# Deferred VectorE work queued behind the low part of its pair of k-blocks, in a hybrid attention and convolution block

## The chip, the cores and the metric

The kernel runs on one core of one Trainium2 chip. The metric is device time in microseconds of that core, from the start of an execution to its end; the median of three runs before the change is 2037.59 us (2037.36 to 2040.66). The engines that matter here are TensorE (PE in the profile: matrix products and transposes; PEld is its weight load), VectorE (DVE: elementwise work), ScalarE (ACT: casts and activations), the DMA queue that SyncE issues (SP) and GpSimd (POOL).

## The reference, cut to what matters

The input has 256 rows and 4096 columns. The projection `w_in` has 14336 columns: q, k, v and z_a (2048 each) for 16 attention heads, and a_c, g_c and z_c (2048 each) for a convolution module.

```python
xn = rms_norm(h, norm_in_g[i])
proj = xn @ w_in[i]
q, k, v, z_a, a_c, g_c, z_c = jnp.split(proj, ...)
y_a = chunked_attention(q, k, v, rel_table[i])
y_a = rms_norm(y_a, attn_out_g[i]) * silu(z_a)
u = a_c * sigmoid(g_c)                      # GLU
u = causal_depthwise_conv(u, w_dw, 31 taps) + b_dw
u = silu(layer_norm(u, ln_g, ln_b))
y_c = u @ w_pw + b_pw
y_c = rms_norm(y_c, conv_out_g[i]) * silu(z_c)
h = h + concatenate([y_a, y_c]) @ w_out[i]
gate = sigmoid(rms_norm(h, ple_norm_g[i]) @ w_ple_gate[i] + b_ple_gate[i])
h = h + gate * (p[i] @ w_ple[i])
out = rms_norm(h, final_g)
```

Everything is float32. The chip's products are made of two parts of each operand, high and low.

## The kernel before

**One k-block of a weight.** A k-block is 128 rows of a weight matrix, loaded as a tile `wt` of 128 x 1024 (two blocks of 512 columns). `parts_of` (lines 199 to 210) makes two operands of it: ScalarE casts `wt` to the high part `wh` (line 204), and VectorE subtracts to get the low part `wl` (line 205). The last pair of instructions made in this way is remembered in the list `recent` (line 209): its first entry is the cast on ScalarE, its second the subtraction on VectorE. There are three buffers each for `wh` and `wl`, and five for `wt`.

**A product.** `mixed_product` (lines 339 to 500) makes two blocks of 512 output columns at once and goes over the 16 pairs of k-blocks in an order written out by hand. A plain pair (no mark) costs VectorE two low parts of 1024 columns, and TensorE 24 matmuls (two k-blocks, two column blocks, two row halves, three part combinations). A pair marked `*` is done with seven products in place of eight, which is 21 matmuls, and needs sums of weight blocks: VectorE makes a low part of 512 columns for `w0`, two additions into `ua` (lines 464, 465), the low part `ul` of `ua`, the low part of `w1`, two more additions into `ub` (lines 471, 472) and the low part of `ub`. In a pair marked `+` the first two additions are made by the DMA on its way in. The products of a seven-pair accumulate in four more PSUM banks (`acc_P`), which are taken from the pool of temporary banks from the first seven-pair to the last.

**Deferred work.** VectorE work that nothing needs at once is put into the queue `later` (line 180) as closures. At the end of every pair, `fill(n)` (lines 182 to 184) takes the next n closures and traces their instructions there; n comes from a list, `fills`, indexed by the pair's place in the order. I say that a closure is *dealt* to the pair after which `fill` traces it. What goes through `later`:

- the convolution: `glu_conv(c)` queues 4 x 31 = 124 taps, each one VectorE instruction on up to 256 columns (lines 714 and 718), for c = 0 to 3, 496 in all. The 31 taps of one channel block are a chain, as each adds to the same `cv`;
- `combinations(c)`: two closures, one of five VectorE instructions (lines 291 and 268 to 271) and one of a cast and a subtraction (lines 276, 277);
- `layer_norm_swish`: sums, means, centring (line 799), squares (line 803 on ScalarE, their additions on line 807), the scaling (line 832), the activation and the split into parts (line 844);
- the gating of `y_a` and `y_c` (line 1031, recorded as line 184), a combination of the last output operand, and, in the gate's products, the multiplication of the embedding's product with the gate, the addition to `hc`, its square (ScalarE) and its weighting (lines 1155 to 1158; recorded as line 184).

**The order of the stages**, with the closures dealt in each: `glu_conv(0)`; then for g = 0, 1, 2: `glu_conv(g + 1)` and `heads(g)`; then `layer_norm_swish` (which only queues) and `heads(3)`. `heads(g)` is a product for q and k, one for v (`product`, lines 235 to 247, fills of 2 at each of 16 pairs), then `attention(g)`, whose small matmuls, softmax and transposes are spread among the first pairs of the next product. The products of `glu_conv(1)`, `glu_conv(2)` and of q and k use

```python
early = units("1 3 5 0+ 7 9 2+ 11 13 4+ 15 8 6+ 10 12 14")
early_fills = (5, 6, 1, 5, 6, 1, 5, 6, 1, 5, 6, 1, 2, 5, 5, 4)
```

(q and k of `heads(3)` with a fill of 4 at every pair), and the product of `glu_conv(3)`, called the last a/g product below, uses

```python
early_six = units("1 3 5 7 0* 9 2* 11 4* 13 6* 15 8* 10* 12 14")
six_fills = (4, 6, 7, 1, 5, 1, 5, 1, 5, 1, 2, 4, 6, 6, 6, 4)
```

where `more_combinations` also puts two combinations at the head of `later`, ahead of pairs 7 and 9. Both lists add up to 64. After the attention come the pointwise product (fills of 0), the z products and `w_out` (2) and the gate's products (4), whose orders are written out in the same way and are mostly `*` pairs.

**What sets the order on an engine.** The order of the instructions on each engine is fixed when the program is built. The framework goes through a list schedule: of the instructions whose inputs it reckons to be there, an engine takes the one traced first. So a closure dealt to a late pair may be placed far ahead of that pair on VectorE, if its inputs are there and nothing traced earlier is. `pin` (line 89) holds an instruction behind the one traced before it on its engine; `queued_behind` (lines 214 to 220) holds what is traced inside it behind given instructions, each on its own engine: an edge of order, not a wait for the other's end. Before the change only the parts of `ua` in `+` pairs use it (line 466), with what `recent` held when the pair began. Each engine executes its instructions in the order so fixed.

Of the kernel before, what the change touches and what calls it, by code (L numbers as in the profile page):

```python
# [25 lines left out]
def hybrid_block(  # L26
# [24 lines left out]
    _, T, D = x.shape  # L51
# [128 lines left out]
    later = deque()  # L180

    def fill(n):
        for _ in range(min(n, len(later))):
            later.popleft()()


    def weight_parts(w, col, k0, kc, tiles=None):
# [24 lines left out]
    recent = []  # L212
# [126 lines left out]
    def mixed_product(  # L339
        w, col, lhs, comb, order, on_helpers, ahead=None, fills=(0,), on_begin=None, apart=NB,  # L340
        left=(), begin=None,
    ):

        c = [[ps_acc.tile([P, NB], F32, tag="acc", name=f"acc{h}{j}") for j in range(2)] for h in range(NH)]  # L350
        helper = {}
        begun, ends = set(), {}
        n_left = len(left) // 2
        for n, (_, seven) in enumerate(order[: len(order) - n_left]):
            for name in ("P1", "P5", "P6", "P7", "P2", "P3", "P4") if seven else ("P2", "P3", "P4", "X"):
                ends[name] = n
        banks = {"P2": c[0][0], "P3": c[0][1], "P4": c[1][0], "X": c[1][1]}
        made, held = [], []

        def add_left(h, js, out=None, cols=slice(None)):  # L360


            for m in range(0, len(held), 2):
                for j in js:
                    dst = c[h][j] if out is None else out[:, cols]
                    for i, (kb, (wh, wl)) in enumerate(held[m : m + 2]):
                        xh, xl = block(kb, h)
                        for kind, (a, b) in enumerate(((xh, wh), (xl, wh), (xh, wl))):
                            pin(
                                nc.tensor.matmul(  # L370
                                    dst, a, b[:, j, cols],
                                    start=out is not None and m + i + kind == 0,
                                    stop=m + i + 1 == len(held) and kind == 2,
                                )
                            )

        def add(name, x, w2, n, final, kinds=range(3), then=lambda ins: None):

            for kind in kinds:
                a, b = ((x[0], w2[0]), (x[1], w2[0]), (x[0], w2[1]))[kind]  # L380
                made.append(
                    nc.tensor.matmul(  # L382
                        banks[name], a, b, start=name not in begun,
                        stop=final and ends[name] == n and kind == 2 and not (left and name in "P2 P3 P4"),
                    )
                )
                begun.add(name)
                then(made[-1])

        def block(kb, h):  # L390
            t = lhs[kb // 4]
            return [t[:, kb % 4, q, h * P : (h + 1) * P] for q in range(2)]

        def add_plain(n, k, wh, wl, **kw):
            pair = order[n][0]
            for j in range(2):
                for h in range(NH):
                    name = (("P2", "P3"), ("P4", "X"))[h][j]
                    add(name, block(2 * pair + k, h), (wh[:, j], wl[:, j]), n, k == 1, **kw)

        sums = {}

        def sums_ahead(n):
            for m in range(n, min(n + 3, len(order))):
                if order[m][1] != "+" or m in sums:
                    continue
                ua = sums[m] = upool.tile([P, 2, NB], F32, tag="u", name="ua")
                rows = w[2 * order[m][0] * P : (2 * order[m][0] + 1) * P, :]
                step = P * rows.ap[0][0]

                def columns(first, step):
                    return bass.AP(
                        tensor=rows.tensor, offset=rows.offset + first,
                        ap=[list(rows.ap[0]), [step, 2], [1, NB]],
                    )

                nc.sync.dma_start(ua, columns(col + apart, 0))
                nc.gpsimd.dma_start(ua, columns(col, step + apart), accum_op=ALU.add)

        done, after = 0, ExitStack()  # L420
        if begin:
            done, behind = begin(add_plain)
            for ins in behind:
                after.enter_context(tc.issue_after(ins.ins))
        last_seven = max((n for n, (_, seven) in enumerate(order) if seven), default=None)
        for n, (pair, seven) in enumerate(order):
            if n < done:
                continue
            if ahead:
                ahead(pair)  # L430
            wts = []
            for k in range(2):
                wt = wpool.tile([P, 2, NB], F32, tag="w", name="wt")
                if seven == "+" and k == 0:
                    nc.sync.dma_start(wt[:, 0], w[2 * pair * P : (2 * pair + 1) * P, col : col + NB])
                else:
                    nc.sync.dma_start(wt, two_columns(w, 2 * pair + k, col, apart))
                wts.append(wt)
            sums_ahead(n)
            if n >= len(order) - n_left:  # L440
                for k in range(2):
                    tiles = left[2 * (n - len(order) + n_left) + k]
                    held.append((2 * pair + k, parts_of(wts[k], 2, tiles and tiles())[0]))
                fill(fills[n % len(fills)])
                continue
            if not seven:
                for k in range(2):
                    add_plain(n, k, *parts_of(wts[k], 2)[0])
                fill(fills[n % len(fills)])
                continue  # L450
            begins = not helper
            if begins:
                for name in ("P1", "P5", "P7", "P6"):
                    helper[name] = ps_tmp.tile([P, NB], F32, tag="tmp", name=f"acc_{name}")
                banks.update(helper)
            w0, w1 = wts
            plus = partial(nc.vector.tensor_tensor, op=ALU.add)
            before = list(recent)
            w0h, w0l = parts_of(w0, 1)[0]
            if seven == "+":  # L460
                ua = ub = sums[n]
            else:
                ua = upool.tile([P, 2, NB], F32, tag="u", name="ua")
                plus(ua[:, 0], w0[:, 0], w0[:, 1])  # L464
                plus(ua[:, 1], w0[:, 1], w1[:, 1])  # L465
            with queued_behind(before if seven == "+" else ()):
                uah, ual = pair_parts(ua)
            w1h, w1l = parts_of(w1, 2)[0]
            if seven != "+":
                ub = upool.tile([P, 2, NB], F32, tag="u", name="ub")  # L470
            plus(ub[:, 0], ua[:, 0], w1[:, 1])
            plus(ub[:, 1], ub[:, 0], w1[:, 0])  # L472
            ubh, ubl = pair_parts(ub)
            first = len(made)

            def s_of(i):
                t, at = comb[pair] if isinstance(comb, dict) else (comb[pair // 4], pair % 4)
                return [t[:, at + i // 2, q, (i % 2) * P : (i % 2 + 1) * P] for q in range(2)]

            k0, k1 = 2 * pair, 2 * pair + 1  # L480
            add("P1", block(k0, 0), (w0h[:, 0], w0l[:, 0]), n, True)
            add("P5", s_of(1), (uah[:, 0], ual[:, 0]), n, True)
            add("P7", s_of(0), (uah[:, 1], ual[:, 1]), n, True)
            add("P2", block(k1, 0), (w1h[:, 0], w1l[:, 0]), n, True)
            add("P3", s_of(3), (w1h[:, 1], w1l[:, 1]), n, True)
            add("P6", s_of(2), (ubh[:, 0], ubl[:, 0]), n, True)
            add("P4", block(k1, 1), (ubh[:, 1], ubl[:, 1]), n, True)
            if begins and on_begin:
                on_begin()
            if begins:  # L490
                tc.add_manual_dep(
                    made[first].ins, last_transpose[0].ins.name,
                    mybir.DependencyInfo(mybir.DependencyClass.NoSync, mybir.DependencyReason.DATA),
                    reason="transposes before the helpers take their banks",
                )
            if n == last_seven:
                on_helpers(helper)
            fill(fills[n % len(fills)])
        after.close()
        return (c, add_left) if left else c  # L500
# [811 lines left out]
```

## Time and profile before

| what | value |
|---|---|
| median of three runs | 2037.59 us (2037.36 to 2040.66) |
| profiled execution, its own time | 2040.98 us |
| its span, from the first to the last instruction | 2039.2 us |
| granted TensorE clock, mean | 0.997 |
| ACT busy | 1198.3 us (59%) |
| mean DMA rate | 211 GB/s |

The profile is of one execution. Busy times are unions of the spans of an engine's instructions. Matmuls are pipelined: one lasts some 390 ns in the records while the next starts 227 ns after it, so a busy share of TensorE of 99% says that it seldom stood still for long, and short waits between matmuls are seen only in the distance of their starts. A row of a timeline gives the start, the time, the engine, the line, the operation, the tiles written and read and a count; in brackets stands the engine's idle time before it and what ended it. A row of the table by windows gives for a stretch the busy time of each engine with the number of its instructions, the granted clock, the share of the DMA engines and the rate.

### The profile page before, as it was taken

The page shows a single profiled execution, that of the slowest core. Times are in us where ns is not written, and L with a number is a line of the kernel's source. Part 1 is how long each engine was busy: PE and PEld are TensorE (multiplying, and loading weights), DVE is VectorE, ACT ScalarE, POOL GpSimd, SP SyncE. Part 2 cuts the span into 40 slices and gives each one's busy share as a digit, 9 for nine tenths or more (in the row PEclk, how much of TensorE's full clock was granted, in tenths as well). Part 3 has the DMA queues.
Part 4 walks back from the last instruction along what each step waited for, and adds up shares of the span by engine and source line. Part 5 has one row for each costly group of instructions (what it writes and reads, how often), then busy time and mean ns, then how long its engine had stood idle before and what let it go on. Part 6 is the DMA issues. An engine that isn't in the chain of part 4 may idle for free.

```text
span 2039.2 us, 26104 instructions
## 1 busy us (share of the span) xinstructions
PE 2019.7 (99%) x9106; PEld 1662.4 (82%) x9106; DVE 1860.4 (91%) x2640; ACT 1198.3 (59%) x1559; POOL 37.5 (2%) x43
## 2 busy tenths in 40 slices
PE   9999999999999999999999999999999999999997
PEld 7888888888888888788888888888888888888876
DVE  7999998699889977868899999999999999999998
ACT  7655446454555545666556566676565666655555
POOL 0000000000000000000000000000000000000000
PEclk9999999999999999999999999999999999999999
DMA  8787866876568866565666666676666656666765
GB/s 292 222 238 234 256 199 180 253 227 187 175 189 265 254 188 204 160 186 203 195 211 201 196 211 200 220 236 204 213 201 205 214 185 207 200 220 204 234 209 177
DMA packets 171839, 431.18 MB, mean 211 GB/s; under 512 B 13742, under 2 KB 16958, under 8 KB 171706
## 3 DMA queue, kind: packets, MB, share of 16 engines
q1 hardware_dynamic: 164528, 416.09, 63.2%
q0 software_dynamic: 6528, 12.58, 3.8%
q8 instruction: 71, 1.16, 0.2%
q10 hardware_dynamic: 650, 0.84, 0.1%
q14 instruction: 62, 0.51, 0.1%
HBM read 425.26 MB, written 4.19 MB: 211 GB/s over the span
## 4 chain that ended last, share of the span: by engine, by line
PE 91%; DVE 6%; issue 2%; DMA 0%; ACT 0%; POOLq 0%; POOL 0%; ACTq 0%; DVEq 0%
PE acc L382 65%; PE acc_P L382 16%; PE acc L229 7%; DVE wl L205 2%; DVE cv L718 2%; PE tmp_ps L170 1%; DMA wt<-in_w_in_dram 0%; PE tmp_ps L890 0%; PE tmp_ps L908 0%; PE tmp_ps L875 0%; PE tmp_ps L913 0%; PE acc L370 0%; PE tmp_ps L125 0%; DVE ul L205 0%; PE tmp_ps L915 0%
## 5 line engine op out<-in xcount | busy, mean ns | idle before, releaser
L382 PE MATMUL acc<-wh,big_t 128*128 128x512 f32 x3788 | 1172.0, 392 | 1.8 <-DVE z L1029 1.1
L204 ACT CAST wh<-wt 128x1024 fp32r<-128x1024 f32 (+1 forms) x737 | 715.7, 980 | 579.0 <-PE acc L382 353.6
L205 DVE TENSOR_TENSOR wl<-wt,wh 128x1024 fp32r<-128x1024 f32 (+1 forms) x737 | 824.5, 1131 | 91.3 <-ACT wh L204 86.0
L382 PEld LDWEIGHTS acc<-wh,big_t 128*128 128x128 f32 x3788 | 708.9, 188 | 149.1 <-ACT wh L204 1.5
L382 PE MATMUL acc<-wl,big_t 128*128 128x512 f32 x1894 | 732.3, 392 | 2.8 <-DVE wl L205 2.8
L382 PEld LDWEIGHTS acc<-wl,big_t 128*128 128x128 f32 x1894 | 355.8, 188 | 77.7 <-DVE wl L205 4.2
L718 DVE SCALAR_TENSOR_TENSOR cv<-uT,dw,cv 128x250 f32<-128x250 f32 (+21 forms) x480 | 200.5, 462 | 1.2
L204 ACT CAST uh<-ua 128x1024 fp32r<-128x1024 f32 x146 | 153.6, 1052 | 67.1 <-DVE ua L465 46.4
L205 DVE TENSOR_TENSOR ul<-ua,uh 128x1024 fp32r<-128x1024 f32 x146 | 177.9, 1218 | 7.6 <-ACT uh L204 7.4
L229 PE MATMUL acc<-wh,big_t 128*128 128x512 f32 x560 | 173.6, 390 | 0.0
L204 ACT CAST uh<-ub 128x1024 fp32r<-128x1024 f32 x98 | 103.1, 1052 | 98.5 <-DVE ub L472 70.6
L382 PE MATMUL acc_P<-uh,big_t 128*128 128x512 f32 x504 | 154.2, 391 | 0.1
L205 DVE TENSOR_TENSOR ul<-ub,uh 128x1024 fp32r<-128x1024 f32 x98 | 119.6, 1221 | 6.7 <-ACT uh L204 6.1
L229 PEld LDWEIGHTS acc<-wh,big_t 128*128 128x128 f32 x560 | 105.1, 188 | 21.6
L382 PEld LDWEIGHTS acc_P<-uh,big_t 128*128 128x128 f32 x504 | 93.5, 188 | 21.9 <-ACT uh L204 3.1
L229 PE MATMUL acc<-wl,big_t 128*128 128x512 f32 x280 | 108.9, 389 | 0.0
L382 PE MATMUL acc_P<-ul,big_t 128*128 128x512 f32 x252 | 96.5, 391 | 0.0
L464 DVE TENSOR_TENSOR ua<-wt 128x512 f32<-128x512 f32 x98 | 67.3, 687 | 22.6 <-DMA wt<-in_w_in_dram 17.0
L382 PE MATMUL acc<-uh,big_t 128*128 128x512 f32 x244 | 75.6, 390 | 0.0
L382 PE MATMUL acc_P<-wh,big_t 128*128 128x512 f32 x244 | 75.3, 389 | 0.0
L465 DVE TENSOR_TENSOR ua<-wt 128x512 f32<-128x512 f32 x98 | 67.1, 685 | 3.2 <-DMA wt<-in_w_in_dram 2.1
L472 DVE TENSOR_TENSOR ub<-ub,wt 128x512 f32<-128x512 f32 x98 | 67.3, 687 | 1.0
(244 smaller groups left out, 1575.6 us busy)
## 6 DMA issues: line engine op xcount, KB each, us to landing
wt<-in_w_in_dram SPq DMA_DIRECT2D x423, 512.0 KB, 4.4
wt<-in_w_out_dram SPq DMA_DIRECT2D x128, 512.0 KB, 4.3
wt<-in_w_ple_gate_dram SPq DMA_DIRECT2D x128, 512.0 KB, 4.1
wt<-in_w_pw_dram SPq DMA_DIRECT2D x32, 512.0 KB, 4.5
ua<-in_w_in_dram SPq DMA_DIRECT2D x24, 512.0 KB, 4.3
ua<-in_w_in_dram POOLq DMA_DIRECT2D x24, 512.0 KB, 8.2
wt<-in_w_in_dram SPq DMA_DIRECT2D x24, 256.0 KB, 2.7
hc<-in_x_dram SPq DMA_DIRECT2D x8, 512.0 KB, 5.3
```

What stands on the lines that cost most here:

```text
L170: nc.tensor.transpose(pt[:, i * T + h * P : i * T + (h + 1) * P], src[:, h, b * P : (b + 1) * P], ident,)
L204: nc.scalar.copy(wh[:, :kc, :], wt[:, :kc, :]),
L205: nc.vector.tensor_tensor(wl[:, :kc, :], wt[:, :kc, :], wh[:, :kc, :].bitcast(F32), ALU.subtract),
L229: nc.tensor.matmul(acc, a, b[:, k, :], start=kb == 0 and kind == 0, stop=kb == kblocks - 1 and kind == 2,)
L382: nc.tensor.matmul(banks[name], a, b, start=name not in begun, stop=final and ends[name] == n and kind == 2 and not (left and name in "P2 ...
L464: plus(ua[:, 0], w0[:, 0], w0[:, 1])
L465: plus(ua[:, 1], w0[:, 1], w1[:, 1])
L472: plus(ub[:, 1], ub[:, 0], w1[:, 0])
L718: nc.vector.scalar_tensor_tensor(cv[:, i, PAD - k :], uT[:, i, : T + k - PAD], dw[:, b, k : k + 1], cv[:, i, PAD - k :], ALU.mult, ALU.add,)
```

## The change

`fill` traces its closures inside `queued_behind(recent[1:])`. The slice leaves the VectorE entry alone, so every VectorE instruction of a closure is held behind the low part that `recent` names; instructions of the closure on other engines are not. In a seven-pair, `recent` is set at the end to the parts of `w1` (kept in `latest`), and not left at those of `ub`; in a plain pair it is the second k-block's. So what is dealt to a pair can be placed no earlier than right behind the low part of that pair's second k-block. In a seven-pair that is ahead of the additions into `ub` and of the low part of `ub`. No instruction is added or removed.

```diff
     def fill(n):
-        for _ in range(min(n, len(later))):
-            later.popleft()()
+        with queued_behind(recent[1:]):
+            for _ in range(min(n, len(later))):
+                later.popleft()()
...
             with queued_behind(before if seven == "+" else ()):
                 uah, ual = pair_parts(ua)
-            w1h, w1l = parts_of(w1, 2)[0]
+            (w1h, w1l), latest = parts_of(w1, 2)
             if seven != "+":
                 ub = upool.tile([P, 2, NB], F32, tag="u", name="ub")
             plus(ub[:, 0], ua[:, 0], w1[:, 1])
             plus(ub[:, 1], ub[:, 0], w1[:, 0])
             ubh, ubl = pair_parts(ub)
+            recent[:] = latest
             first = len(made)
```

The `+` pairs, which read `recent` when they begin, always follow a plain pair in `early`, so their own edge stays as it was.

## The prediction

> **What bounds the kernel now.** I read the page first, then the windows of the taps' line, then the stretches in which VectorE is late or full.
>
> ```profile
> span 2039.2 us, 26104 instructions
> PE 2019.7 (99%) x9106; PEld 1662.4 (82%) x9106; DVE 1860.4 (91%) x2640; ACT 1198.3 (59%) x1559; POOL 37.5 (2%) x43
> ...
> L718 DVE SCALAR_TENSOR_TENSOR cv<-uT,dw,cv 128x250 f32<-128x250 f32 (+21 forms) x480 | 200.5, 462 | 1.2
> ```
>
> TensorE stands idle for 2039.2 - 2019.7 = 19.5 us in all, its warm-up and every softmax included: that is about all that a better order could win. A worse order has no such lid, since VectorE is busy for 91% and feeds TensorE an operand for every third matmul. The taps are the bulk of what is deferred: 200.5 us over 480 instructions, 0.42 us each when they run back to back.
>
> Where do they run? The window query for their line says:
>
> ```profile
> 102.00:137.00 35.00, 14.21 (x33) 1.00 0.78 218
> ...
> 259.00:310.00 51.00, 28.63 (x72) 1.00 0.67 199
> ...
> 355.00:405.00 50.00, 0.00 (x0) 1.00 0.87 252
> ...
> 525.00:575.00 50.00, 3.08 (x7) 1.00 0.57 170
> 575.00:625.00 50.00, 0.00 (x0) 1.00 0.71 227
> ```
>
> The second stretch is a product for v: 2 taps are dealt to a pair of 24 matmuls, 5.4 us, so some 19 in 51 us; 72 ran. The last two rows hold the last a/g product, to which (below) 52 taps are dealt; 7 ran. So the scheduler places taps far ahead of where they are dealt, and the edges must move them. That the change does nothing is thereby excluded.
>
> **The change part by part.** It removes and adds no instruction. It moves VectorE work from stretches before to stretches where it is dealt, and I price each place by what VectorE has left there.
>
> *Last a/g product.* Before it, 3 x 124 = 372 taps have been queued and 64 + 64 + 32 + 64 + 64 + 32 = 320 dealt; 52 are left, and the two combinations come on top. By `six_fills` its pairs get: first three 17 taps; then one combination's five instructions; its last one and 4 taps; the second's five; its last and 4 taps; then 1, 5, 1, 2, 4, 6, 6, 2 taps. What VectorE does there now:
>
> ```profile
> 560.00:616.00 56.00, 56.00 (x252) 46.33 (x252) 45.58 (x53) 34.11 (x41) 0.00 (x0) 1.00 0.63 197
> ...
> 600.00:610.00 10.00, 10.00 (x46) 8.29 (x45) 9.93 (x13) 5.49 (x7) 0.00 (x0) 1.00 0.69 212
> ```
>
> ```profile
> L464 DVE TENSOR_TENSOR ua<-wt 128x512 f32<-128x512 f32 x5 | 3.5, 691 | 5.8 <-DMA wt<-in_w_in_dram 5.8
> ```
>
> ```profile
> L291 DVE TENSOR_TENSOR comb<-big_t 128x512 f32<-128x512 f32 x2 | 1.3, 674 | 0.0
> ...
> L268 DVE TENSOR_TENSOR comb<-comb 128x128 f32<-128x128 f32 x2 | 0.5, 274 | 0.0
> ```
>
> (The third number of busy times in the first view is VectorE's: 45.58 of 56 us. The second view is its groups in 560 to 616, the third those in 490 to 560, where both combinations begin now.) A combination's first closure costs 0.67 + 4 x 0.27 = 1.75 us, its second another addition of that size, 0.67. From the fourth pair to the thirteenth, up to the last seven, that deals 2 x (1.75 + 0.67) + 27 taps x 0.42 = 16.2 us (the six of the pair 10* itself come behind its sums). VectorE has 56 - 45.6 = 10.4 us free there, of which 5.8 us are waits for a weight whose buffer VectorE's own additions set free, so taps placed ahead of those additions delay the transfer too. Its lead at the end is small:
>
> ```profile
> 608.50 2.96 DVE L205 TENSOR_TENSOR wl<-wt,wh 128x1024 fp32r<-128x1024 f32 x3
> ...
> 614.06 1.22 DVE L205 TENSOR_TENSOR ul<-ub,uh 128x1024 fp32r<-128x1024 f32 x1
> ```
>
> ```profile
> 610.28 0.61 PE L382 MATMUL acc<-wh,big_t 128*128 128x512 f32 x2
> 610.74 0.39 PE L382 MATMUL acc<-wl,big_t 128*128 128x512 f32 x1
> ...
> 616.86 0.39 PE L382 MATMUL acc_P<-ul,comb_x 128*128 128x512 f32 x1
> ```
>
> The low part of `w1` in 8* ends at 608.50 + 1.22 = 609.72, and TensorE takes it at 610.74: 1.0 us. The last `ul` ends at 615.28 and is taken at 616.86: 1.6 us. If all free time can be used, TensorE waits 16.2 - 10.4 - 1.6 = 4.2 us; if the time behind the transfer can't, 5.8 more, 10.0 us. Behind a tap wait the next low parts and sums on VectorE, TensorE for these, and the next transfer for their buffers. I take the middle, 7 us, since of these stretches the one at 600 has no free time left (9.93 of 10) and the earlier ones some.
>
> *The early products.* Three pairs (24 + 24 + 21 matmuls at (610.74 - 610.28) / 2 = 0.23 us, 15.7 us) are dealt 12 taps. The stretch 102 to 137 ran 33 in 35 us, 14.8 in that time, so VectorE copes. But the taps there stand where they are dealt, right behind the first convolution's end, and at the second `+` pair TensorE waits:
>
> ```profile
> 135.72 0.39 PE L382 MATMUL acc_P<-uh,comb_t 128*128 128x512 f32 x1
> 136.28 0.50 PE L382 MATMUL acc_P<-ul,comb_t 128*128 128x512 f32 x1 [0.17 <-DVE ul L205]
> 136.61 0.39 PE L382 MATMUL acc<-uh,big_t 128*128 128x512 f32 x1
> ```
>
> ```profile
> 665.39 0.39 PE L382 MATMUL acc<-uh,big_t 128*128 128x512 f32 x1
> 665.80 0.50 PE L382 MATMUL acc_P<-ul,comb_t 128*128 128x512 f32 x1
> 666.14 0.39 PE L382 MATMUL acc<-uh,big_t 128*128 128x512 f32 x1
> ```
>
> 0.33 + 0.10 us beyond 0.23 the first time, 0.18 + 0.11 the second (the q and k of `heads(2)`, where the queue had run dry and begins anew in the same way). The other four products of this order would now get the same pattern: 4 x 0.43 = 1.7 us. Bounds: 0, and 0.43 at three of the four `+` pairs of six products less the two paid, 18 x 0.43 - 0.7 = 7.0.
>
> *Attention.* The second and third attention now run with few taps beside them:
>
> ```profile
> 316.00:345.00 29.00, 28.85 (x147) 23.48 (x146) 25.06 (x51) 21.33 (x45) 1.21 (x1) 1.00 0.49 144
> 537.00:562.00 25.00, 25.00 (x131) 20.15 (x131) 18.54 (x35) 19.30 (x41) 0.00 (x0) 1.00 0.50 147
> 758.00:783.00 25.00, 25.00 (x131) 20.10 (x130) 18.07 (x33) 18.30 (x40) 0.30 (x1) 1.00 0.54 172
> ```
>
> They get 17 and about 16 taps, 7 us: from 18.5 to 25 of 25 us. The first has them already, at 25.06 of 29, and there TensorE shows 0.15 us idle, which is the lower bound for each. The upper bound is what does not fit if VectorE can use only the first attention's share (25.06 / 29 of 25 us = 21.6): 25.3 - 21.6 = 3.7, less a lead of 1.6 to 2, some 2 us each. I take 0.5 each, 1 us.
>
> *The gate's products.* Four multiplications `z<-acc,z` are dealt to the first pair; now some precede its second low part:
>
> ```profile
> 1758.23 1.28 DVE L184 TENSOR_TENSOR z<-acc,z 128x512 f32<-128x512 f32 x2
> 1759.43 0.68 DVE L465 TENSOR_TENSOR ua<-wt 128x512 f32<-128x512 f32 x1
> 1760.03 0.68 DVE L184 TENSOR_TENSOR z<-acc,z 128x512 f32<-128x512 f32 x1
> 1760.63 1.22 DVE L205 TENSOR_TENSOR wl<-wt,wh 128x1024 fp32r<-128x1024 f32 x1
> ...
> 1845.57 0.68 DVE L184 TENSOR_TENSOR z<-acc,z 128x512 f32<-128x512 f32 x1
> 1846.33 1.23 DVE L205 TENSOR_TENSOR wl<-wt,wh 128x1024 fp32r<-128x1024 f32 x1
> ```
>
> ```profile
> 1759.18 1.64 ACT L204 CAST wh<-wt 128x1024 fp32r<-128x1024 f32 x2
> ```
>
> The cast for that low part can't end before 1760.2. Behind the edge VectorE has only line 465 (0.68) from 1758.23 on and stands idle for some 1.3 us; in the next product one multiplication, 0.6 us, moves, and I take the last for the same. VectorE's rows show no idle time around it, so nothing makes this good: 1.3 + 0.6 + 0.6 = 2.5 us at most, none if the lead covers it; I take 1.5.
>
> *At nothing:* the layer norm. Its mean, its centring and its splits wait for each other rather than for a place:
>
> ```profile
> 832.51 0.48 PE L787 MATMUL tmp_ps<-lnsum,mean_w 128*128 128x256 f32 x1
> ...
> 846.05 0.80 PE L382 MATMUL acc<-wl,big_t 128*128 128x512 f32 x1 [2.84 <-DVE wl L205]
> ```
>
> ```profile
> 834.58 3.10 DVE L799 TENSOR_TENSOR cv<-cv,mu 128x256 f32<-128x256 f32 x9
> ...
> 844.77 2.36 DVE L205 TENSOR_TENSOR wl<-wt,wh 128x1024 fp32r<-128x1024 f32 x2
> ```
>
> The mean's matmul takes a temporary bank, and these are held until the sums of the last seven-pair, the thirteenth, are read out. What is dealt ahead of it (28 taps at 4 to a pair, then four closures) ends with the eighth pair, so 832 stays. The centring then comes in a burst, behind low parts that are already past. If that cover goes, the mean comes later and the burst with it, at no other price.
>
> The sum: 7 + 1.7 + 1 + 1.5 = 11.2 us. The profiled execution took 2040.98 us, 1.8 beyond its span and 3.4 above the median, so it would become 2052.2, and the median of the runs 2037.59 + 11.2 = 2048.8 us.
>
> [...] In the window 830 to 860 the granted clock is lower, and behind the wait of 2.84 us matmuls start 0.43 us apart for a while:
>
> ```profile
> 830.00:860.00 30.00, 27.16 (x125) 22.20 (x124) 26.60 (x43) 18.47 (x24) 0.72 (x1) 0.94 0.47 141
> ```
>
> By that row a new wait of such a length costs 0.06 x 30 = 1.8 us more; I count it for none of mine, as I expect several of 1 to 3 us. [...]
>
> **The rivals.** *It is hidden.* VectorE's sums are made ahead: if the whole 10.4 us and the 1.6 us of lead are used, and the first seven's earlier lead too, the last a/g product costs 0 to 4 and the rest 1: 2037.6 to 2041, say 2039.5. For it: the wait for the transfer, 5.8 us, stands right behind the sums of a seven-pair, where taps would come. Against: the 600 to 610 stretch is full without a single tap.
>
> *Faster: the centring's burst breaks up.* If the new order puts one centring between two low parts, in place of nine in a row, the wait at 846.05 (2.84 us) and its slow clock (1.8) go: 4.6 us, 2033.0, if nothing above costs. It decides from where the other costs sum to less than 4.6 us. Against: the burst begins 2 us behind the mean, and the edges only hold back.
>
> *VectorE becomes the bound of all these stages.* Upper ends together: 10.0 + 7.0 + 4 + 2.5, and the slow clock once, 1.8: 25 us, 2063. For it: the order is fixed, so one late tap delays every operand behind it. Against: the 33 taps in 35 us.
>
> **How the numbers follow.** My forecast 0.56, hidden 0.22, faster 0.10, bound 0.12. A measurement of this kernel can tell 0.2%, 4.1 us, from no change. Faster by more than that: the burst's case and little else, 0.11. Within: the hidden case and the low edge of the forecast, 0.24. Slower: 0.65. The forecast's own range is 2042 to 2058; with half of the hidden case and part of the large one, 2036 to 2060.
>
> **What would show it.** Right: in the taps' windows some 20 where 72 ran, about 30 and 20 in the last two rows; VectorE at 55 or more of the 56 us of the last a/g product's sevens, with new idle time of TensorE put down to `wl` or `ul` there, 4 to 10 us; 0.4 us at the second `+` pair of each early product; the three or four `z` in a row behind the low part in the gate's products; the wait at 846 unchanged. Wrong: taps moved but TensorE's starts in the last a/g product unbroken (then the lead was larger than the two rows show), or time lost where nothing was dealt.

## The result, and the profile after

| | before | after |
|---|---|---|
| median of 16 runs each | 2039.33 us (2037.34 to 2040.66) | 2042.91 us (2040.64 to 2044.99) |
| ratio, 95% interval | | 1.0018 [1.0011, 1.0024] |
| profiled execution, its own time | 2040.98 us | 2040.64 us |
| its span | 2039.2 us | 2038.9 us |
| granted TensorE clock, mean | 0.997 | 0.998 |

The change makes the kernel 3.6 us slower; 11.2 us were forecast. The two profiled executions do not show that difference in their spans, since the one before is 1.6 us above its median and the one after is the lowest of its sixteen runs. So the places have to be read one by one. Line numbers after the change are up to two higher: the casts are line 205, the low parts 206, the additions 465, 466, 472 and 473, the taps 720.

The head of the page after the change: TensorE busy in the same number of matmuls, and VectorE 15 us busier with the same 2640 instructions. One tap lasts as long as before (464 ns and 462), but the busy time is the union of the records: in a row these overlap, and a tap adds 0.42 us to it, while a tap that stands apart adds its whole 0.46.

```profile
span 2038.9 us, 26091 instructions
...
PE 2018.2 (99%) x9106; PEld 1660.6 (81%) x9106; DVE 1875.6 (92%) x2640; ACT 1199.4 (59%) x1559; POOL 37.5 (2%) x43
...
L720 DVE SCALAR_TENSOR_TENSOR cv<-uT,dw,cv 128x255 f32<-128x255 f32 (+15 forms) x480 | 221.1, 464 | 6.2
```

The windows of the taps' line after (VectorE's busy time and count, then clock, DMA share and rate):

```profile
259.00:310.00 51.00, 18.03 (x39) 1.00 0.69 201
...
525.00:575.00 50.00, 12.44 (x27) 1.00 0.57 168
575.00:625.00 50.00, 11.97 (x26) 1.00 0.62 192
```

The taps moved as the edges say: 39 where 72 ran in the product for v, and 27 and 26 where 7 and none ran. The windows of all engines in the same stretches, with the second attention (the third busy time is VectorE's):

```profile
259.00:310.00 51.00, 51.00 (x234) 42.34 (x234) 42.00 (x64) 21.14 (x23) 0.00 (x0) 1.00 0.69 201
...
537.00:562.00 25.00, 25.00 (x131) 20.02 (x130) 22.74 (x50) 19.06 (x43) 0.00 (x0) 1.00 0.47 140
...
560.00:616.00 56.00, 55.27 (x243) 44.86 (x241) 55.77 (x89) 32.62 (x40) 0.00 (x0) 1.00 0.61 184
```

VectorE has 9 us free in the product for v, where nothing needs them, and works 55.77 of 56 us in the sevens of the last a/g product, 10.2 us more than before. Its waits for a weight there are gone, as its groups of 560 to 616 show (last column: idle time ahead of the group, 5.8 us before):

```profile
L720 DVE SCALAR_TENSOR_TENSOR cv<-uT,dw,cv 128x230 f32<-128x230 f32 (+26 forms) x27 | 12.4, 460 | 0.0
...
L465 DVE TENSOR_TENSOR ua<-wt 128x512 f32<-128x512 f32 x5 | 3.4, 681 | 0.0
```

TensorE's timeline after, 606 to 632, the rows that show idle time:

```profile
616.64 1.19 PE L383 MATMUL acc_P<-uh,comb_x 128*128 128x512 f32 x4 [1.37 <-ACT uh L205]
620.92 0.73 PE L383 MATMUL acc_P<-uh,comb_x 128*128 128x512 f32 x2 [1.26 <-ACT uh L205]
628.93 1.19 PE L383 MATMUL acc<-wl,big_t 128*128 128x512 f32 x4 [0.43 <-DVE wl L206]
```

These are the new waits. A matmul's record lasts 0.39 us and the next normally starts 0.23 after its start, so each wait is 0.16 longer than its bracket says: 1.53 + 1.42 + 0.59 = 3.5 us. The two long ones name ScalarE's cast, which is not what was late. ScalarE's rows say what it waited for:

```profile
615.54 1.04 ACT L205 CAST uh<-ua 128x1024 fp32r<-128x1024 f32 x1 [0.44 <-DVE ua L466]
...
619.82 1.04 ACT L205 CAST uh<-ub 128x1024 fp32r<-128x1024 f32 x1 [1.29 <-DVE ub L473]
```

And VectorE's rows of the same time, none with idle time ahead of it, show why its sums were late:

```profile
613.48 0.45 DVE L720 SCALAR_TENSOR_TENSOR cv<-uT,dw,cv 128x236 f32<-128x236 f32 x1
613.85 0.68 DVE L465 TENSOR_TENSOR ua<-wt 128x512 f32<-128x512 f32 x1
614.45 0.45 DVE L720 SCALAR_TENSOR_TENSOR cv<-uT,dw,cv 128x235 f32<-128x235 f32 x1
614.83 0.68 DVE L466 TENSOR_TENSOR ua<-wt 128x512 f32<-128x512 f32 x1
...
618.07 0.68 DVE L472 TENSOR_TENSOR ub<-ua,wt 128x512 f32<-128x512 f32 x1
618.68 0.45 DVE L720 SCALAR_TENSOR_TENSOR cv<-uT,dw,cv 128x233 f32<-128x233 f32 x1
619.05 0.68 DVE L473 TENSOR_TENSOR ub<-ub,wt 128x512 f32<-128x512 f32 x1
```

In these rows a tap stands ahead of each pair of sums or between its two. The chain that sets the end at this place is VectorE's sums, then ScalarE's cast, then the matmul. Summed over all matmuls that start in 600 to 650 us, what the distances of successive starts have beyond 0.227 us (called lost starts below) is 4.5 us after and 0.2 before: 4.3 us more.

Elsewhere the change gives a little back. TensorE's rows at the second `+` pair after the change:

```profile
135.95 0.39 PE L383 MATMUL acc_P<-ul,comb_t 128*128 128x512 f32 x1
136.18 0.62 PE L383 MATMUL acc<-uh,big_t 128*128 128x512 f32 x2
```

The 0.43 us of before are gone, and so is the like wait at 665: together 0.7 us. So 4.3 - 0.7 = 3.6 us, the difference of the medians. That the two spans are nearly alike is a matter of these two executions: in the one before, the wait of the layer norm was followed by a lowered clock (1.7 us, last section), and the lost starts between 950 and 1450, stages that the theory below does not touch, are 2.7 us more than in the one after.

### The profile page after: what moved, and what is told of

Read it like the earlier page. It is cut to its first block, busy times and chain, and to the rows that moved or that the text cites. A ratio compares the mean times of both kernels' runs of the same rounds, so it can differ in the third digit from the quotient of the medians.

```text
span 2038.9 us, 26091 instructions
## 1 busy us (share of the span) xinstructions
PE 2018.2 (99%) x9106; PEld 1660.6 (81%) x9106; DVE 1875.6 (92%) x2640; ACT 1199.4 (59%) x1559; POOL 37.5 (2%) x43
## 4 chain that ended last, share of the span: by engine, by line
PE 94%; DVE 3%; issue 1%; ACT 1%; DMA 0%; POOLq 0%; POOL 0%; ACTq 0%; DVEq 0%
PE acc L383 66%; PE acc_P L383 16%; PE acc L230 9%; DVE wl L206 1%; PE tmp_ps L170 1%; DVE ul L206 1%; PE tmp_ps L877 0%; PE tmp_ps L892 0%; DVE cv L720 0%; PE tmp_ps L910 0%; PE tmp_ps L915 0%; DMA wt<-in_w_ple_dram 0%; DVE hc L185 0%; PE tmp_ps L125 0%; DVE ub L472 0%
## 5 line engine op out<-in xcount | busy, mean ns | idle before, releaser
L720 DVE SCALAR_TENSOR_TENSOR cv<-uT,dw,cv 128x255 f32<-128x255 f32 (+15 forms) x480 | 221.1, 464 | 6.2
```

Of the source, the lines that this page charges most:

```text
L720: nc.vector.scalar_tensor_tensor(cv[:, i, PAD - k :], uT[:, i, : T + k - PAD], dw[:, b, k : k + 1], cv[:, i, PAD - k :], ALU.mult, ALU.add,)
```

## The experiments

The theory was: the last a/g product alone makes the loss, because VectorE gets more there than it has time for, and the early products give a little back. The rivals were that the loss is spread over all stages, and that it is the new place of the edge in a seven-pair, ahead of the additions into `ub`, that counts and not the amount of work. The first four kernels ran together, with 11 runs each beside 33 of the kernel before at 2038.54 us.

**The edges in the last a/g product alone.** A flag, False at the start, says where `fill` sets its edges.

```diff
-        with queued_behind(recent[1:]):
+        with queued_behind(recent[1:] if held_behind[0] else ()):
...
+            held_behind[0] = last
             sg, gate = scaled_pair(
...
+            held_behind[0] = False
```

> The edges of fill are kept in the last a/g product alone; everywhere else closures are placed freely as before the change. If the cost lies in that product (16 us of closures against 10 us of free VectorE time), its taps come back to it and TensorE waits there as with the whole change, whose three new waits of 1.54, 1.43 and 0.59 us with their tails make 3.9 us: 3 to 5 us slower than before. If the cost is spread over all stages, 0 to 2 us slower.

Measured: 2042.46 us, ratio 1.0019 [1.0010, 1.0028], that is 3.9 us slower. The three waits are back, their brackets the same to the hundredth of a microsecond (TensorE's timeline of this kernel, rows with idle time, 600 to 650; its lines are one higher still):

```profile
616.63 1.19 PE L384 MATMUL acc_P<-uh,comb_x 128*128 128x512 f32 x4 [1.37 <-ACT uh L206]
620.91 0.73 PE L384 MATMUL acc_P<-uh,comb_x 128*128 128x512 f32 x2 [1.26 <-ACT uh L206]
628.92 1.20 PE L384 MATMUL acc<-wl,big_t 128*128 128x512 f32 x4 [0.43 <-DVE wl L207]
```

**The edges everywhere but there.** The same flag, True at the start, `not last` ahead of that product and True again behind it.

> The edges are kept everywhere but in the last a/g product, whose 52 taps and two combinations may again float ahead. If the cost lies in that product: no new wait there, and the waits of 0.43 and 0.29 us at the second + pair that the whole change took away stay away, so 0.2 to 1 us faster than before. If the cost is spread: 2 to 4 us slower.

Measured: 2038.19 us, ratio 0.9997 [0.9988, 1.0006], 0.35 us below before, which the interval cannot tell from no change. The timeline of TensorE here from 600 to 650 has no row with idle time, and VectorE in the sevens is back near its 45.58 us (windows of this kernel):

```profile
560.00:616.00 56.00, 56.00 (x252) 46.30 (x251) 47.41 (x56) 33.96 (x42) 0.00 (x0) 1.00 0.61 194
```

By the medians the two halves add up to the whole: 3.9 - 0.35 = 3.6 us. So the loss lies in one product, and the attention, the early products and the gate's products together cost nothing that these runs can tell (-2.4 to +1.2 us).

**The edge behind `ub`'s low part.** The line that moves `recent` back to `w1`'s parts is left out, so what is dealt to a seven-pair comes behind the low part of `ub` and no longer between its sums.

```diff
             ubh, ubl = pair_parts(ub)
-            recent[:] = latest
```

> The whole change without its second part: in a seven-pair the closures queue behind the low part of ub, not behind that of w1. If the amount of work dealt to the last a/g product decides, the same 16 us meet the same free time: 3 to 5 us slower than before, with the waits there between 3 and 5 us in sum. If it is the place that decides (taps put between the two additions into ub, ahead of the cast that TensorE waits for), the waits on the cast of ua and ub fall below 1 us in sum and the time is within 1 us of before.

Measured: 2042.79 us, ratio 1.0022 [1.0013, 1.0031], no better than after. TensorE's rows with idle time between 600 and 650:

```profile
616.00 0.49 PE L383 MATMUL acc<-wl,big_t 128*128 128x512 f32 x1 [0.29 <-DVE wl L206]
620.68 0.74 PE L383 MATMUL acc_P<-uh,comb_x 128*128 128x512 f32 x2 [1.56 <-ACT uh L205]
628.71 1.21 PE L383 MATMUL acc<-wl,big_t 128*128 128x512 f32 x4 [0.44 <-DVE wl L206]
...
```

The waits sit a pair elsewhere and come to the same sum (lost starts 4.1 us above before in 600 to 650, against 4.3). Of these two places of the edge within a pair neither is the better one; VectorE's order only chooses which operand is late.

**Less dealt ahead of the last sevens.** Sixteen closures that were dealt to the pairs 15, 8* and 10* go to the two plain pairs behind the last seven-pair.

```diff
-six_fills = (4, 6, 7, 1, 5, 1, 5, 1, 5, 1, 2, 4, 6, 6, 6, 4)
+six_fills = (4, 6, 7, 1, 5, 1, 5, 1, 5, 1, 2, 0, 0, 0, 9, 9)
```

> The whole change with the last five fills of the last a/g product (4, 6, 6, 6, 4) made (0, 0, 0, 9, 9): the same number of closures in that product, but none dealt to the pairs 15, 8* and 10*, and 18 to the two plain pairs at its end. Up to the last sevens 16.2 - 10 taps x 0.42 = 12.0 us are then dealt, against 10.4 us free and 1.6 us of lead. If all free time can be used, as the lower bound of the forecast had it, the waits of 1.54 and 1.43 us go, and at most 1.5 us come back at the product's end, where 7.6 us of taps meet the sums: 0 to 2 us slower than before. If the time behind the transfers can't be used (5.8 us), 4 to 6 us of waits stay.

Measured: 2039.03 us, ratio 1.0004 [0.9995, 1.0012]: the loss is gone but for what the interval leaves open. The two long waits are gone, though VectorE is busy for 55.81 of 56 us in the window 560 to 616 of this kernel. One wait of 0.76 us is there, at 641, where the closures run that were moved:

```profile
641.40 1.19 PE L383 MATMUL acc<-wl,big_t 128*128 128x512 f32 x4 [0.60 <-DVE wl L206]
```

The lost starts between 600 and 650 are 1.3 us above before, in place of 4.3; less the 0.7 us given back, that is the 0.5 us between the medians. The same edges and the same work, sixteen taps later in the product: what costs is the amount dealt ahead of the last seven-pair.

**The product for v takes more.** The 9 us that VectorE has free in each product for v are the place from which the edges took the taps. Two such products lie ahead of the last a/g product, so with three closures at a step instead of two, 32 taps fewer are left for it: 20 of 52. (Run with the next kernel; 11 runs each beside 21 of the kernel before at 2038.99 us.)

```diff
-        accv = product(w_in0, o_v + g * NB, xT, KD)
+        accv = product(w_in0, o_v + g * NB, xT, KD, fills=3 if g < n_g - 1 else 2)
```

> The whole change with 3 closures in place of 2 dealt to each of the 16 steps of the product for v in heads 0, 1 and 2 (a step there is one block of columns, 12 matmuls, 2.7 us). That takes 32 taps out of the last a/g product: 20 are left, 8.4 us, with 4.8 us of combinations. If the amount dealt against the free time decides, its new waits go below 0.5 us in sum, and the time is 0 to 1 us faster than before. If edges cost something wherever they stand, 2 to 4 us slower remain. What could come in their place: the product for v, whose VectorE share was 42 of 51 us after the change, gets 16 taps or 7 us more and has no room beyond that.

Measured: 2040.68 us, ratio 1.0011 [1.0002, 1.0020]: slower than before by 1.7 us. The waits at 616 to 629 are indeed gone, with VectorE at 48.77 of 51 us in the product for v and 53.22 of 56 in the sevens:

```profile
560.00:616.00 56.00, 56.00 (x249) 46.39 (x248) 53.22 (x70) 34.46 (x40) 0.00 (x0) 1.00 0.67 208
259.00:310.00 51.00, 51.00 (x234) 42.41 (x233) 48.77 (x79) 21.14 (x23) 0.00 (x0) 1.00 0.67 198
```

But the layer norm behind it got worse, which I had not foreseen. TensorE's rows around it in this kernel:

```profile
831.23 0.70 PE L789 MATMUL tmp_ps<-lnsum,mean_w 128*128 128x256 f32 x2
843.01 1.20 PE L383 MATMUL acc<-wl,big_t 128*128 128x512 f32 x4 [1.05 <-DVE wl L206]
...
848.27 0.50 PE L383 MATMUL acc<-wl,big_t 128*128 128x512 f32 x1 [1.39 <-DVE wl L206]
849.18 0.71 PE L829 MATMUL tmp_ps<-lnsum,mean_w 128*128 128x128 f32 x4 [0.41 <-DVE lnsum L828]
```

The third product for v also takes 16 taps more, so 12 are queued in place of 28 when the last q and k begins, and the layer norm's closures are dealt four pairs earlier. The mean still gets its temporary bank no earlier than 831, once the seven-pairs' sums are read out, and by then more of what hangs on it has been dealt. VectorE's row right behind it:

```profile
833.29 4.11 DVE L801 TENSOR_TENSOR cv<-cv,mu 128x256 f32<-128x256 f32 x12
```

Twelve centrings in a row, then squares' additions of 1.22 us each, and the low parts late behind them, where the kernels before and after have one wait near 846 or 850. Between 800 and 870 us this kernel has 6.9 us of lost starts, with no lowered clock among them (it reads 1.00 in the windows 800 to 830, 830 to 860 and 860 to 905); before has 5.4, of which 1.7 are the lowered clock. So of the 4.3 us that the last a/g product is relieved of, 3.2 come back here.

**The mean ahead of the seven-pairs.** If the bank is what the mean waits for, it has to come before the first seven-pair of that product, which is the fourth in the order. With 12 taps and the four sums ahead of it, 6, 6 and 5 closures at the first three pairs reach it. `rest` holds four closures that do nothing and serves as a pause; behind the spread it is made four times as long.

```diff
-        q, k = scaled_pair(w_in0, o_q + g * NB, o_k - o_q, early, r_x, (4,) if g == n_g - 1 else early_fills)
+        q, k = scaled_pair(w_in0, o_q + g * NB, o_k - o_q, early, r_x, (6, 6, 5) + 13 * (4,) if g == n_g - 1 else early_fills)
...
         later.append(lambda: spread(st["s"]))
-        later.extend(rest)
+        later.extend(rest * 4)
```

This comes on top of the edit for v.

> As v_three, and in heads 3 the fills (6, 6, 5, then 4), so that the mean's matmul is dealt to the third pair, ahead of the first seven-pair, which takes the four temporary banks; and twelve more empty closures ahead of the scaling, so that it comes after the banks are free. If the wait of 3.0 us near 846, which all kernels so far show, comes from the mean waiting for a bank and the centring then coming in a burst, the centring spreads over the pairs and that wait goes, with the slow clock after it: 3 to 5 us faster than before. If the burst comes from elsewhere, a wait of 2.5 to 3 us stays near 846 and the time is within 1 us of before. The variance and the scaling still wait for the banks and could burst in turn: then a wait of 1 to 2 us.

Measured: 2035.38 us (2034.13 to 2036.34), ratio 0.9983 [0.9974, 0.9992]: 3.6 us faster than before. TensorE's timeline of this kernel has the mean right ahead of the first matmul into `acc_P`:

```profile
785.96 0.59 PE L789 MATMUL tmp_ps<-lnsum,mean_w 128*128 128x256 f32 x2
786.20 0.81 PE L383 MATMUL acc_P<-wh,big_t 128*128 128x512 f32 x2
...
834.08 0.68 PE L829 MATMUL tmp_ps<-lnsum,mean_w 128*128 128x128 f32 x4 [0.44 <-DVE lnsum L828]
```

The last row is the only one between 800 and 862 that shows idle time; the wait of 2.8 us that before and after have there is gone. The window:

```profile
830.00:860.00 30.00, 29.56 (x141) 24.15 (x140) 21.81 (x34) 24.79 (x42) 0.72 (x1) 1.00 0.59 173
```

TensorE is busy for 29.56 of 30 us, where before it was 27.16 at a clock of 0.94. That the mean waited for a bank, and not for its turn in the queue, shows beside the kernel before it: dealt four pairs sooner it came at 831.23 in place of 832.51, and dealt ahead of the first seven-pair it came at 785.96. The new fills and the longer pause came in one edit; how much each does for the wait is not separated.

**The same dealing without the edges.** Does the gain need the edges? Both edits of the dealing, in the kernel before (11 runs beside 15 of before at 2038.59 us).

> The dealing of mean_first (three taps to a pair in the v products of the first three groups of heads, 6, 6 and 5 closures at the first pairs of the last q and k, the rest four times as often behind the spread) in the kernel before the change, with no edge. Theory (the dealing alone lets the mean have its bank before the first seven-pair takes the temporary banks; the edges have no part in the gain): the mean's matmul stands ahead of the first acc_P of that product, the 3.0 us wait near 846 is gone, and the only loss against mean_first is the wait of some 0.4 us at each of two + pairs: 2035 to 2037, ratio 0.998 to 0.999. Rival (the edges are needed, since without them VectorE takes the work of the layer norm in bursts wherever its inputs are there, ahead of low parts): the mean is early too, but the centring comes as a row of ten ahead of a low part and TensorE waits 1 to 3 us there: 2037 to 2040, ratio 0.9995 to 1.0005.

Measured: 2035.39 us (2034.6 to 2037.01), ratio 0.9986 [0.9977, 0.9995]. The rival falls: the mean is at 786.45 here too, and the window of this kernel is like the last one:

```profile
830.00:860.00 30.00, 29.54 (x141) 24.19 (x140) 26.63 (x48) 27.82 (x50) 0.73 (x1) 1.00 0.57 174
```

The edges have no part that can be measured in this gain. The waits at the two `+` pairs, 0.7 us, are in this profile and not in the one with edges, but the two medians are 0.01 us apart and the two ratios' intervals overlap almost wholly; whether the edges are worth that on top stays open. Nor was the dealing of the last q and k tried without the edit for v.

## Why the prediction was right and wrong

It was right in direction and in the place that decides, and too large by a factor of three. By its terms, with the lost starts of TensorE in place of the forecast terms:

| term | predicted | measured |
|---|---|---|
| last a/g product | +7 (4.2 to 10.0) | +4.3; alone 3.9 by the medians |
| second `+` pairs of the early products | +1.7 (0 to 7.0) | -0.7 |
| attention | +1 (0.3 to 4) | 0 |
| the gate's products | +1.5 (0 to 2.5) | +0.2 |
| layer norm | 0 | 0 |
| sum | 11.2 | 3.8; 3.6 by the medians |

Of the 7.4 us that the terms have too much, 2.7 lie in the last a/g product, 2.4 in the early products, 1.0 in the attention and 1.3 in the gate's products. So no single term explains the miss: with the lower bound for the last a/g product the sum would still have been 8.4. In three of them the step that failed is the same: moved work was charged to TensorE although VectorE had idle time, or other work that was ready, where it went. In the early products a wait that came from work taken too early was read as one from work placed too late. The runs show the new waits of TensorE in one product alone, where VectorE has no free time left.

The measured 2042.91 us does lie in the forecast's own range, 2042 to 2058, and that is luck: the range was counted from a median of three runs, 2037.59, and the median of sixteen is 1.7 us higher. Counted as a change, its lower end is 4.4 us, above the 3.6 measured. By the prediction's yardstick of 4.1 us a change of 3.6 is none, a case that got a chance of 0.24; sixteen runs each do tell it from none.

*Last a/g product, the largest term.* "I take the middle, 7 us, since of these stretches the one at 600 has no free time left (9.93 of 10) and the earlier ones some." What is dealt there was counted rightly: 27 taps were forecast between the fourth pair and the thirteenth, and 27 ran in the stretch. So was the free time, 10.4 us: VectorE is now 10.2 us busier there. What failed is the choice between the bounds. The lower one, 16.2 - 10.4 - 1.6 = 4.2 us, lets VectorE use all its free time, the 5.8 us behind the weight's transfer among it, and this is what happened: that idle time is 0.0 after, and with sixteen closures fewer ahead of the last sevens VectorE is as full and neither long wait is left. That 4.2 and 4.3 are so near each other is in part chance: 0.7 of the 4.3 is lost behind the last seven-pair, which the count leaves out. I argued that taps ahead of the additions delay the transfer as well; but a wait of VectorE for a transfer was time in which the tap ran at no cost. That the transfer which it makes later had slack of the same kind at the next pair is an inference from the idle time that vanished; no run isolates it. The releasers were also misnamed: the two long waits are for `uh`, by way of ScalarE's cast of a late sum, and not for `wl` or `ul`.

*The early products.* The sign was wrong. I took the wait at 136 for the mark of taps that stand where they are dealt, and so expected it at four more places. It is the opposite, as VectorE's rows before show:

```profile
132.75 1.21 DVE L718 SCALAR_TENSOR_TENSOR cv<-uT,dw,cv 128x232 f32<-128x232 f32 x3
133.88 1.21 DVE L205 TENSOR_TENSOR wl<-wt,wh 128x1024 fp32r<-128x1024 f32 x1
135.01 1.21 DVE L205 TENSOR_TENSOR ul<-ua,uh 128x1024 fp32r<-128x1024 f32 x1
```

Three taps in a row, and a low part of the next pair, stand ahead of `ul`; that the taps were taken there because their inputs were ready is read from how the schedule is made. Behind the edges the same taps come one by one behind later low parts, and `ul` is 3.4 us earlier:

```profile
131.58 1.22 DVE L206 TENSOR_TENSOR ul<-ua,uh 128x1024 fp32r<-128x1024 f32 x1
132.72 0.45 DVE L720 SCALAR_TENSOR_TENSOR cv<-uT,dw,cv 128x232 f32<-128x232 f32 x1
133.20 1.22 DVE L206 TENSOR_TENSOR wl<-wt,wh 128x1024 fp32r<-128x1024 f32 x1
```

So an edge of order also does what the text before gave it no credit for: it keeps work that is ready from being taken too early.

*Attention.* VectorE rose to 22.74 of 25 us in the second one and to 19.35 in the third, not to 25; TensorE stayed at 25.00 busy in both, and the kernel with the edges everywhere but in the last a/g product is no slower for it.

*The gate's products.* The multiplications moved behind the second low part, as forecast; the idle time that this was to leave did not come. VectorE's rows after, between the two low parts, none with idle time:

```profile
1757.75 0.68 DVE L466 TENSOR_TENSOR ua<-wt 128x512 f32<-128x512 f32 x1
1758.35 0.68 DVE L472 TENSOR_TENSOR ub<-ua,wt 128x512 f32<-128x512 f32 x1
1759.07 0.69 DVE L473 TENSOR_TENSOR ub<-ub,wt 128x512 f32<-128x512 f32 x1
```

The two additions into `ub`, which need only `ua` and the weights, took the place. I had looked for cover in the rows around the moved work, and not for other work of the same pair that was ready.

*The layer norm* was priced at nothing, and the wait is the same, 3.0 us, 4 us later (849.86 for 846.05):

```profile
849.86 0.50 PE L383 MATMUL acc<-wl,big_t 128*128 128x512 f32 x1 [2.83 <-DVE wl L206]
```

The reason given, a bank that the seven-pairs hold, is what the kernel with the mean ahead of them shows. I counted a lowered clock for none of the new waits, and that held as well: the trace after has it at 1.00 from 5.5 us of the span to 2029.6.

*The product for v.* 19 taps were forecast where 39 ran: a step of that product is one column block, 12 matmuls, not 24, so two closures come in 2.7 us. No term of the sum hung on this, but it left me blind to how much the products for v could still take: after the change 9 us each.

*The rivals.* "It is hidden" said that the whole 10.4 us and the lead are used and put the last a/g product at 0 to 4; the mechanism is what the traces show, and 4.3 lies just above its upper end. It had a chance of 0.22, the forecast 0.56. "VectorE becomes the bound" falls: TensorE waits anew in one product alone. "Faster" did not come by the edges, but its price was near: the edits of the dealing that take the burst apart gain 3.2 to 3.6 us, where 4.6 had been reckoned with a slow clock that not every execution has (last section).

## What to carry to other kernels

Where work is moved onto an engine that has little time left, count what it is given against what it has free, stretch by stretch, and believe the count: here the idle time in front of a transfer, 5.8 us before and 0.0 after, was free time like any other. Before a term is read from a wait in the trace, look at what stands ahead of the late instruction and whence it came: the same wait can mean that work was placed too late or too early. And a wait that no order of the engine removes may be for a resource, here a bank, whose holder can be overtaken by dealing the work some pairs sooner: the wait of 3.0 us is gone in the kernel whose mean runs at 785.96 and not at 832.51.

## What was not expected of the hardware

The layer norm's wait of 3.0 us is the same in the kernels before, after and of the first four experiments, but what the granted clock does behind it is not. The windows of the kernel before (behind the five busy times stand the clock, the DMA share and the rate):

```profile
845.00:855.00 10.00, 8.95 (x34) 7.39 (x35) 7.86 (x10) 3.51 (x4) 0.72 (x1) 0.83 0.70 211
```

After the change:

```profile
845.00:855.00 10.00, 7.17 (x32) 5.59 (x32) 9.92 (x15) 6.39 (x7) 0.00 (x0) 1.00 0.37 108
```

With the edges in the last a/g product alone:

```profile
845.00:855.00 10.00, 7.17 (x22) 5.41 (x21) 9.94 (x14) 5.45 (x7) 0.00 (x0) 0.72 0.33 106
855.00:865.00 10.00, 10.00 (x56) 8.64 (x55) 6.61 (x13) 4.61 (x7) 0.73 (x1) 0.94 0.49 157
```

In windows that lie wholly inside these stretches the clock reads 0.50, and the matmuls of the kernel before start 0.43 us apart there (847.07 to 849.20), in place of 0.23. A clock at half speed for a time t takes t / 2 off a longer window. So before, t is 2 x 0.17 x 10 = 3.4 us; after, nothing; and in the third kernel 2 x (0.28 + 0.06) x 10 = 6.8 us. In windows of 0.2 us it is 3.41 us in three of the six kernels, 6.82 and 6.83 us in two and nothing in one, a profile each. The next table sets the stretch of the lowered clock, read from the windows of 0.2 us, beside the wait, which is counted from the time at which the next matmul was due.

| kernel | wait (us) | clock at 0.50 (us) | clock lowered for |
|---|---|---|---|
| before | 843.05 to 846.05 | 846.08 to 849.50 | 3.41 |
| less dealt ahead of the last sevens | 844.83 to 847.82 | 847.97 to 851.38 | 3.41 |
| edges everywhere but there | 842.99 to 845.99 | 846.78 to 850.20 | 3.41 |
| edge behind `ub` | 847.08 to 850.07 | 849.46 to 856.29 | 6.83 |
| edges in the last a/g product alone | 847.04 to 850.03 | 849.31 to 856.14 | 6.82 |
| after | 846.87 to 849.86 | none | 0 |

In three of these six executions the clock falls behind the end of the wait, by 0.03, 0.15 and 0.79 us. In two it falls while TensorE still stands, 0.61 and 0.72 us ahead of the end, and there it stays low for twice as long. In one, after a wait of the same length, it does not fall. Half of the time at 0.50 that lies behind the end of the wait, an estimate from the table, is what the wait cost besides itself: 1.7 us in three executions, 3.1 us in two and nothing in one. So the length of the wait, 3.0 us in all six, does not say what the clock does; what does is left open here. A single profile is thus good for the places of the waits, and not for differences of the span of a few us.
